# Moving the modulation products between the six sub-layers of a diffusion step

## The chip, the cores and the metric

The kernel runs on one core of a Trainium2 chip. The time is that of one execution on the device, in microseconds (us); several executions are timed and their median is given. One more execution was taken with the hardware profiler, and all rows below come from it. PE is TensorE (PEld its weight loads), DVE VectorE, ACT ScalarE, POOL GpSimd, and SP the engine whose queue issues nearly all of the DMA transfers.

## The reference

Two layers of a diffusion backbone, each with three sub-layers: a half-step SwiGLU feed-forward, a token mixer, and a second half-step feed-forward. There are 512 latent and 128 context tokens of width 1024, all in float32. The mixer of the first layer is a real 2-D Fourier transform over positions and channels (8 groups of 128 channels) between an input and an output projection; that of the second is a 16-head attention, dense among the context tokens and local in a grid for the latent ones. Each sub-layer is wrapped in norms whose shift, scale and gate come from a modulation vector:

```python
def _modulation(cond, w_mod, b_mod):
    m = jax.nn.silu(cond) @ w_mod + b_mod
    return m.reshape(cond.shape[0], N_MOD, D_MODEL)

def _modulated_prenorm(x, g, m, k):
    return _rmsnorm(x, g) * (1 + m[:, 3 * k + 1, None]) + m[:, 3 * k, None]
```

So each layer has nine modulation vectors of 1024 (three for each sub-layer), for two conditions (latent and context). The matrix `w_mod` of a layer is 1024 x 9216, 36 MB, and each of its numbers is used once for each condition. This work depends only on the two condition vectors and can be done at any time before the sub-layer that uses it.

## The kernel before, in words

All activations are kept transposed (128 channels on the partitions, tokens along the free axis) and the 640 tokens are handled as two halves of 320. For accuracy every float32 operand is split into a high part (ScalarE, a rounding copy, lines 190 and 200) and a low part (VectorE, the difference, lines 191 and 201), and each product is three matmuls, high x high, high x low, low x high: `mm3`, lines 206 to 208. In the trace a low part is thus a DVE row of L191 (a weight, 128x1024) or of L201 (an activation), and it must be there before its matmul.

Weights come as units of 512 KB (128x1024) by DMA into one of four buffers of the tag `raw` (`NRAW = 4`), are split into `hi` and `lo` tiles (six of each), and the buffer is free again after both. Units are requested in a fixed order (`unit`, three ahead). Tiles of one tag are handed out in program order. The order of instructions on each engine is laid down when the kernel is built: earlier lines of the program have priority, `high_priority` raises a few, and later work may run ahead where its operands and buffers are there. On the chip each engine then works through its list in that order.

The modulation vectors beyond the first two are cut into 128 jobs (`run`, line 1145). One job loads a 512 KB block of the transposed `w_mod` into a `raw` buffer, the same four buffers that the weights use, and has VectorE form two products, one for each condition:

```python
        for cond in conds:
            last = self.nc.vector.scalar_tensor_tensor(
                out=self.junk, in0=raw, scalar=1.0, in1=self.wide[:, cond, :],
                op0=ALU.mult, op1=ALU.mult, accum_out=self.mod[:, layer, cond, j : j + 1])
```

In the trace these are the DVE rows of L336 (`junk<-raw,wide`), and their loads the SP rows `raw<-in_w_mod_t`. Each eighth job adds the few 8-element operations of `coefs`. The jobs stand in one list, and `behind(n)` (line 194) takes the next n of them at that place of the program. Where it is called:

- In a feed-forward layer (`ffn`) the 22 blocks of hidden channels are cut into five slices (`SLICES`). After the first matrix of a slice come its 16 products with the second matrix (`w2`), eight output blocks for each half. `BEHIND[n]` jobs are spread evenly over the 64 `w2` steps of the first four slices (lines 654 to 658). Sub-layers 0, 2, 3 and 5 are feed-forward layers.
- In the Fourier sub-layer (n = 1, `fourier`), the input projection runs in four groups of four output blocks (first half, then second half), with two jobs after each. After each group of the second half `fold` prepares sums and differences of mirrored positions on VectorE (lines 784 to 789). Then come eight rounds, one for each channel group: `channels(g + 1)` (small float32 matmuls, lines 826 to 830; their result is split into the high part by ACT L200 and the low part by DVE L201, `ring<-score`) and `positions(g)` (twelve `mm3` matmuls with the transform matrices, then DVE L851 to L855 and a second split, `ring<-y`). After each of the first six rounds stands one job, and one more after each of the first six blocks of the first half of the output projection (`out_proj`).
- In the attention (n = 4, `attend`), 42 steps are woven between the projections' matmuls, and 24 of the first 33 steps carry a job.

Of the kernel before, what the change touches and what calls it, by code (L numbers as in the profile page):

```python
# [20 lines left out]
NCH = D // P  # L21
# [19 lines left out]
NBLK = 20  # L41
SLICES = ((0, 4), (4, 8), (8, 12), (12, 16), (16, 22))
FAST = range(4, NF - 2)
BEHIND = (28, 20, 28, 28, 24, 0)
BANKS = {"main": 4, "score": 2, "turn": 1, "sum": 1}
TEMPS = {"square": (2, TOK), "total": (2, TOK), "rms": (2, 3 * P), "left": (4, 384), "right": (3, 384)}

# [61 lines left out]
class Kernel:  # L109
# [371 lines left out]
    def ffn(self, layer, which, base, boundary):  # L481
# [3 lines left out]
        n = layer * 3 + 2 * which  # L485
        begun = [False, False]
        g, sums, kept = {}, {}, {}
# [6 lines left out]
        def w1(fs, half):  # L494
            for f in fs:
                if f not in g:
                    g[f] = self.ring(F32R).rearrange("p (a t) -> p a t", a=2)
            pss = []
            if fs[0] >= NF - 2:
                pss = [late(fs[0], j, half) for j in range(2)]  # L500
            elif len(fs) == 1:
                for j in range(2):
                    pss.append(self.proj(self.unit(base + self.w1_at[fs[0]] + j), lambda k: k * P, half,
                                         kind="score" if fs[0] == 2 else "main"))
            else:
                pss = self.multi([self.unit(base + self.w1_at[f] + j) for f in fs for j in range(2)], half)
            for i, f in enumerate(fs):
                gate, up = pss[2 * i], pss[2 * i + 1]
                s, v = self.temp("left"), self.temp("right")
                with self.tc.high_priority():  # L510
                    if f in kept and half:
                        for j, (to, ps) in enumerate(((s, gate), (v, up))):
                            nc.vector.tensor_tensor(to[:, :HALF], ps[:, :HALF], kept[f][j], op=ALU.add)
                        nc.scalar.activation(s[:, :HALF], s[:, :HALF], AF.Silu)
                        nc.vector.tensor_tensor(v[:, :HALF], v[:, :HALF], s[:, :HALF], op=ALU.mult)
                    else:
                        nc.scalar.activation(s[:, :HALF], gate[:, :HALF], AF.Silu)
                        nc.vector.tensor_tensor(v[:, :HALF], up[:, :HALF], s[:, :HALF], op=ALU.mult)  # L518
                    hidden(f, v, half)
                while self.later:  # L520
                    self.later.pop()()
# [23 lines left out]
        def combine(step):  # L545

            if step == 0:
                if n:
                    self.spilled = [self.dram.tile([P, 2 * TOK], F32, tag=f"spill{c}", name=self.name("spill"))
                                    for c in range(NCH // 2)]  # L550
                    for c in range(NCH // 2):
                        nc.sync.dma_start(out=self.spilled[c], in_=self.xs[n][c].rearrange("p c t -> p (c t)"))
                combine.now = {}
            k = step % 2 * 2
            b11, b12, b21, b22 = (self.pair(self.y, c, half) for c in (k, 4 + k) for half in (0, 1))
            if step < 2:
                t = combine.now[k] = [self.temp(("square", "total")[step]).rearrange("p (c t) -> p c t", c=2)
                                      for _ in range(2)]
                steps = ((1, t[0], b12, b11), (2, t[1], b22, t[0]))
            else:  # L560
                t = combine.now[k]
                steps = ((3, t[0], b22, b12), (4, t[1], t[1], b21))
            for i, to, a, b in steps:
                if k == 0:
                    sums[i] = [quad(self.ring(F32R)) for _ in range(2)]
                nc.vector.tensor_tensor(to, a, b, op=ALU.subtract)
                self.split(sums[i][0][:, k : k + 2, :], sums[i][1][:, k : k + 2, :], to)
# [48 lines left out]
        def seed(s, half, m):  # L616

            lo, hi = SPAN[half]
            ps = seeded[s, half, m] = self.bank()
            with self.tc.high_priority():  # L620
                nc.scalar.activation(ps[:, :HALF], self.y[:, m, lo:hi], AF.Copy)  # L621

        def w2(s, half, m):
            f0, f1 = SLICES[s]
            lo, hi = SPAN[half]
            ps = seeded.pop((s, half, m), None) or self.bank()
            for f in range(f0, f1):
                u, a = self.w2_tile(s, m, f - f0)
                w = self.unit(base + u)
                self.mm3(ps[:, :HALF], w[0][:, a : a + P], w[1][:, a : a + P],  # L630
                         g[f][:, 0, lo:hi], g[f][:, 1, lo:hi], f == f0 and s == 0, f == f1 - 1, s > 0)
            with self.tc.high_priority():
                nc.scalar.activation(self.y[:, m, lo:hi], ps[:, :HALF], AF.Copy)  # L633
            if f1 == NF:
                acc[half] = self.weigh(layer, 2 * which, half, m, acc[half])

        passed = done = 0
        adds = [(a[0], half, a[1]) for op, a, half in self.ffn_plan if op == "w2" and a[0]]
        for op, a, half in self.ffn_plan:
            if op == "w2" and a[0]:  # L640
                while adds and len(seeded) < 2 and adds[0][0] == a[0]:
                    seed(*adds.pop(0))
            if op == "w1":
                if not begun[half]:
                    self.finish(half)
                    begun[half] = True
                w1(a, half)
            elif op == "combine":
                combine(a)
            elif op == "fast":  # L650
                w1_fast(a)
            elif op == "w2":
                w2(a[0], half, a[1])
                if a[0] < len(SLICES) - 1:
                    passed += 1
                    due = BEHIND[n] * passed // (2 * NCH * (len(SLICES) - 1))
                    self.behind(due - done)
                    done = due
            elif op == "x":
                self.new_x(n + 1)  # L660
                for c in range(NCH // 2):
                    src = self.spilled[c].rearrange("p (c t) -> p c t", c=2) if n else self.io["x"][:, 2 * c : 2 * c + 2, :]
                    nc.sync.dma_start(out=self.xs[n + 1][c], in_=src)
            else:
                boundary(half, acc[half])
# [99 lines left out]
    def fourier(self, base, boundary):  # L765
# [38 lines left out]
        for half in (0, 1):  # L804
            lo, hi = SPAN[half]
            self.finish(half)
            for m0 in (0, 4):
                pss = self.multi([self.unit(base + m) for m in range(m0, m0 + 4)], half)
                with self.tc.high_priority():
                    for m, ps in zip(range(m0, m0 + 4), pss):  # L810
                        nc.scalar.activation(self.y[:, m, lo:hi], ps[:, :HALF], AF.Copy)
                if half:
                    fold(m0, nc.vector)
                self.behind(2)
        even_w, odd_w = self.unit(base + NCH), self.unit(base + NCH + 1)
        vs = {}

# [42 lines left out]
        for g in range(NCH):  # L860
            if g + 1 < NCH:
                channels(g + 1)
            positions(g)
            if g < 6:
                self.behind()
        self.out_proj(0, base + NCH + 2, boundary)

    def weave(self, parts, ns):
# [174 lines left out]
    def attend(self, pairs, ctx_qk, v):  # L1043
# [75 lines left out]
        for n in range(len(blocks) + 2):  # L1119
            parts = []  # L1120
            if 1 <= n <= len(blocks):
                parts.append(partial(scale, *blocks[n - 1]))
            if n < len(blocks):
                c, b = blocks[n]
                parts += [partial(ctx_scores if b == "c" else scores, c, b, p0) for p0 in range(2)]
            if n >= 2:
                parts.append(partial(take, *blocks[n - 2]))
            if 1 <= n <= len(blocks):
                parts += [partial(turn, *blocks[n - 1], p0) for p0 in range(2)]
            if n < 35 and (n % 5 < 3 or n in (3, 8, 13)):  # L1130
                parts.append(self.behind)
            steps.append(parts)
        return steps
# [143 lines left out]
```

## Time and profile before

| | us |
|---|---|
| median of 3 runs | 2336.14 (2333.36 to 2336.28) |
| the profiled execution's own time | 2334.2 |
| its span, first to last instruction | 2332.4 |
| PE busy | 2278.2 (98%) |
| PEld busy | 2225.2 (95%) |
| DVE busy | 1686.6 (72%) |
| ACT busy | 1270.9 (54%) |
| mean granted TensorE clock | 0.993 of full |

A busy engine is one that executes an instruction; a PE row's duration holds the time that the matmul spends in the pipeline, so consecutive rows overlap, and the rate is read from their starts. The share over the whole span is a mean over stages that differ: the Fourier sub-layer lies at about 480 to 650 us, the attention at about 1550 to 1830.

### The profile page before, as it was taken

The numbers are of one execution on the slowest core, as the hardware profiler recorded it, in microseconds if no ns is written. First come the engines' busy times: TensorE is split into PE (matmuls) and PEld (weight loads), VectorE is DVE, ScalarE is ACT, GpSimd is POOL, SyncE is SP. The second block draws the span as 40 slices with busy tenths as digits, with TensorE's granted clock in tenths as the row PEclk, the third lists the DMA queues.
The fourth block names the chain that finished last, engine by engine and source line by source line (L and its number), as shares of the span: only waits on it lengthen the run. The fifth ranks groups of instructions, "written<-read, shape, count | busy, mean of one in ns | idle before, by whom it ended". The sixth has DMA issues, their size and how long they took to land.

```text
span 2332.4 us, 39397 instructions
## 1 busy us (share of the span) xinstructions
PE 2278.2 (98%) x15756; PEld 2225.2 (95%) x15756; DVE 1686.6 (72%) x2934; ACT 1270.9 (54%) x2448; POOL 45.4 (2%) x64
## 2 busy tenths in 40 slices
PE   6999999998999999999999999999999999999997
PEld 4999999997999999999999999998888899999997
DVE  4878877389788877847878887378877485765553
ACT  4445545564653545556545555567767664545554
POOL 0000000000000000000000000010000000000000
PEclk9999999999999999999999999999999999999998
DMA  8234434334423433443234434224543212221241
GB/s 300 82 115 139 145 118 136 109 103 153 146 99 112 152 109 127 136 154 109 82 125 129 145 118 144 101 81 149 162 135 106 86 73 82 93 89 64 82 136 46
DMA packets 80280, 278.13 MB, mean 119 GB/s; under 512 B 8800, under 2 KB 15200, under 8 KB 79968
## 3 DMA queue, kind: packets, MB, share of 16 engines
q1 hardware_dynamic: 79824, 275.29, 36.1%
q8 instruction: 123, 2.02, 0.4%
q14 instruction: 61, 0.50, 0.1%
q10 hardware_dynamic: 272, 0.33, 0.0%
HBM read 264.04 MB, written 11.53 MB: 118 GB/s over the span
## 4 chain that ended last, share of the span: by engine, by line
PE 88%; DVE 5%; ACT 3%; DMA 3%; issue 1%; POOL 0%; SPq 0%; DVEq 0%; ACTq 0%; POOLq 0%
PE main L206 25%; PE main L208 25%; PE main L207 25%; PE score L206 3%; PE score L208 3%; PE score L207 3%; DVE junk L336 1%; PE sum L1108 1%; PE turn L1092 1%; PE sum L419 1%; DVE lo L191 1%; ACT hi L190 1%; PE score L1066 1%; DMA first<-in_w_mod_k 1%; DMA raw<-in_w_mod_t 1%
## 5 line engine op out<-in xcount | busy, mean ns | idle before, releaser
L206 PE MATMUL main<-ring,hi 128*128 128x320 f32 x3872 | 1204.5, 312 | 3.9 <-ACT ring L200 2.9
L208 PE MATMUL main<-ring,lo 128*128 128x320 f32 x3872 | 1198.0, 310 | 1.6 <-DVE lo L191 1.6
L207 PE MATMUL main<-ring,hi 128*128 128x320 f32 x3872 | 1198.9, 310 | 0.2 <-DVE ring L201 0.2
L206 PEld LDWEIGHTS main<-ring,hi 128*128 128x128 f32 x3872 | 727.7, 188 | 10.0 <-ACT ring L200 3.8
L208 PEld LDWEIGHTS main<-ring,lo 128*128 128x128 f32 x3872 | 727.6, 188 | 2.2 <-DVE lo L191 1.9
L207 PEld LDWEIGHTS main<-ring,hi 128*128 128x128 f32 x3872 | 728.1, 188 | 1.4 <-DVE ring L201 0.9
L190 ACT ACTIVATE hi<-raw 128x1024 fp32r<-128x1024 f32 (+1 forms) x358 | 350.3, 981 | 457.7 <-PE main L207 384.2
L191 DVE TENSOR_TENSOR lo<-raw,hi 128x1024 fp32r<-128x1024 f32 (+1 forms) x358 | 402.6, 1126 | 153.7 <-ACT hi L190 152.5
L336 DVE SCALAR_TENSOR_TENSOR junk<-raw,wide 128x1024 bf16<-128x1024 f32 x256 | 312.4, 1220 | 21.2 <-DMA raw<-in_w_mod_t 18.6
L633 ACT ACTIVATE y<-main 128x320 f32<-128x320 f32 x320 | 138.5, 433 | 172.3 <-PE main L208 170.9
L372 DVE TENSOR_TENSOR total<-total,square 128x640 f32<-128x640 f32 x71 | 58.3, 823 | 108.0 <-ACT square L371 106.1
L621 ACT ACTIVATE main<-y 128x320 f32<-128x320 f32 x256 | 111.9, 439 | 27.2 <-DVE left L607 10.5
L206 PE MATMUL score<-ring,hi 128*128 128x320 f32 x384 | 118.8, 309 | 0.0
L207 PE MATMUL score<-ring,hi 128*128 128x320 f32 x384 | 118.7, 309 | 0.0
L208 PE MATMUL score<-ring,lo 128*128 128x320 f32 x384 | 118.7, 309 | 0.0
L191 DVE TENSOR_TENSOR lo<-sums,hi 128x1024 fp32r<-128x1024 f32 x64 | 78.1, 1221 | 51.1 <-ACT hi L190 51.1
L206 PE MATMUL main<-ring,ring 128*128 128x320 f32 x352 | 110.5, 315 | 0.0
L208 PE MATMUL main<-ring,ring 128*128 128x320 f32 x352 | 108.9, 309 | 0.0
L207 PE MATMUL main<-ring,ring 128*128 128x320 f32 x352 | 108.7, 309 | 0.0
L190 ACT ACTIVATE hi<-sums 128x1024 fp32r<-128x1024 f32 x64 | 67.9, 1061 | 26.4 <-PE main L207 20.5
L200 ACT ACTIVATE ring<-right 128x320 fp32r<-128x320 f32 x112 | 51.6, 467 | 50.6 <-DVE right L518 40.6
L593 DVE TENSOR_TENSOR left<-left,main 128x320 f32<-128x320 f32 x64 | 31.2, 487 | 60.6 <-PE main L208 60.6
(181 smaller groups left out, 2676.1 us busy)
## 6 DMA issues: line engine op xcount, KB each, us to landing
raw<-in_w SPq DMA_DIRECT2D x264, 512.0 KB, 3.6
raw<-in_w_mod_t SPq DMA_DIRECT2D x128, 512.0 KB, 3.7
raw<-in_qkv SPq DMA_DIRECT2D x26, 512.0 KB, 3.7
first<-in_w_mod_k SPq DMA_DIRECT2D x16, 512.0 KB, 8.7
spill<-ring SPq DMA_DIRECT2D x12, 640.0 KB, 3.6
ring<-spill SPq DMA_DIRECT2D x12, 640.0 KB, 4.8
raw<-in_bias SPq DMA_DIRECT2D x16, 448.0 KB, 3.7
raw<-in_four_in SPq DMA_DIRECT2D x8, 512.0 KB, 3.5
```

What stands on the lines that cost most here:

```text
L190: nc.scalar.activation(hi, raw[:, at], AF.Copy)
L191: nc.vector.tensor_tensor(lo, raw[:, at], hi.bitcast(F32), op=ALU.subtract)
L200: self.nc.scalar.activation(hi, src, AF.Copy)
L206: mm(out, whi, xhi, start=start, stop=False)
L207: mm(out, whi, xlo, start=False, stop=False)
L208: self.latest = mm(out, wlo, xhi, start=False, stop=stop)
L336: last = self.nc.vector.scalar_tensor_tensor(out=self.junk, in0=raw, scalar=1.0, in1=self.wide[:, cond, :], op0=ALU.mult, op1=ALU.mult, ac ...
L372: nc.vector.tensor_tensor(acc, acc, sq, op=ALU.add)
L419: self.spread = nc.tensor.matmul(ps[:, t : t + P], col[:, j : j + 1].to_broadcast([P, P]), self.ident, start=True, stop=True)
L593: tt(a, q, z, op=ALU.subtract)
L621: nc.scalar.activation(ps[:, :HALF], self.y[:, m, lo:hi], AF.Copy)
L633: nc.scalar.activation(self.y[:, m, lo:hi], ps[:, :HALF], AF.Copy)
```

## The change

The jobs are the same and in the same order. Their places change: by sub-layer 36, 12, 28, 32, 12 and 8 instead of 28, 20, 28, 28, 24 and 0. In the feed-forward layers the steps of the last slice's first half take part too (72 steps instead of 64, but not in the last layer). In the Fourier sub-layer the input projection's groups carry none in the first half and three each in the second, the rounds none, the output projection six as before. In the attention every third step carries one.

```diff
-BEHIND = (28, 20, 28, 28, 24, 0)
+BEHIND = (36, 12, 28, 32, 12, 8)
...
                 w2(a[0], half, a[1])
-                if a[0] < len(SLICES) - 1:
+                if a[0] < len(SLICES) - 1 or half == 0:
                     passed += 1
-                    due = BEHIND[n] * passed // (2 * NCH * (len(SLICES) - 1))
+                    due = min(BEHIND[n], BEHIND[n] * passed // (2 * NCH * (len(SLICES) - 1) + (NCH if n < 5 else 0)))
                     self.behind(due - done)
                     done = due
...
                 if half:
                     fold(m0, nc.vector)
-                self.behind(2)
+                    self.behind(3)
...
             if g + 1 < NCH:
                 channels(g + 1)
             positions(g)
-            if g < 6:
-                self.behind()
...
-            if n < 35 and (n % 5 < 3 or n in (3, 8, 13)):
+            if n < 35 and n % 3 == 0:
                 parts.append(self.behind)
```

## Rows read from the trace of the kernel before

**Rows 1.** Stages: length; PE, PEld, DVE, ACT, POOL busy (instructions); clock; DMA share, GB/s.
```profile
37.00:482.00 445.00, 441.48 (x2999) 440.03 (x2999) 335.07 (x526) 234.49 (x414) 3.51 (x3) 0.99 0.38 124
482.00:544.00 62.00, 61.30 (x420) 60.49 (x419) 53.66 (x93) 29.61 (x54) 2.21 (x2) 1.00 0.37 117
544.00:582.00 38.00, 29.53 (x223) 26.37 (x222) 36.88 (x85) 20.16 (x50) 0.00 (x0) 0.91 0.41 132
...
1090.00:1548.00 458.00, 457.35 (x3131) 455.92 (x3130) 353.83 (x562) 243.96 (x444) 7.65 (x9) 1.00 0.39 125
...
1584.00:1820.00 236.00, 229.46 (x1771) 205.04 (x1770) 192.00 (x537) 177.17 (x463) 8.97 (x24) 1.00 0.46 144
...
1880.00:2332.00 452.00, 439.45 (x2988) 437.59 (x2987) 263.24 (x398) 225.74 (x405) 7.24 (x6) 0.99 0.25 83
```
**Rows 2.** The same view of the middle of the Fourier stage, in three pieces.
```profile
548.00:566.00 18.00, 15.06 (x127) 13.19 (x127) 17.63 (x43) 9.01 (x23) 0.00 (x0) 1.00 0.36 116
566.00:574.00 8.00, 4.40 (x36) 4.00 (x35) 8.00 (x21) 4.50 (x9) 0.00 (x0) 1.00 0.28 98
574.00:582.00 8.00, 6.07 (x31) 5.77 (x31) 7.25 (x19) 3.56 (x7) 0.00 (x0) 0.57 0.48 146
```
**Rows 3.** Waits in 525 to 600: total us, times, longest.
```profile
PE main L208 <- DVE ring L201: 8.0, 6, 1.9
```
**Rows 4.** VectorE's timeline: start, us, line, operation, tiles.
```profile
543.99 1.23 DVE L336 SCALAR_TENSOR_TENSOR junk<-raw,wide 128x1024 bf16<-128x1024 f32 x1
...
549.18 1.28 DVE L201 TENSOR_TENSOR ring<-score,ring 128x512 fp32r<-128x512 f32 x2
...
559.30 0.68 DVE L201 TENSOR_TENSOR ring<-score,ring 128x512 fp32r<-128x512 f32 x1
...
560.95 1.21 DVE L336 SCALAR_TENSOR_TENSOR junk<-raw,wide 128x1024 bf16<-128x1024 f32 x1
...
562.09 0.68 DVE L201 TENSOR_TENSOR ring<-y,ring 128x512 fp32r<-128x512 f32 x1
562.69 1.21 DVE L336 SCALAR_TENSOR_TENSOR junk<-raw,wide 128x1024 bf16<-128x1024 f32 x1
...
563.84 0.68 DVE L201 TENSOR_TENSOR ring<-score,ring 128x512 fp32r<-128x512 f32 x1
...
582.60 0.34 DVE L855 SCALAR_TENSOR_TENSOR ring<-main,col,ring 128x128 fp32r<-128x128 f32 x1
```
**Rows 5.** PE's timeline, in brackets the idle time before a row and its releaser.
```profile
544.46 0.47 PE L826 MATMUL score<-ring,y 128*128 128x128 f32 x2
...
549.91 0.39 PE L208 MATMUL main<-hi,ring 128*128 128x258 f32 x1 [0.28 <-DVE ring L201]
...
560.04 0.39 PE L208 MATMUL main<-hi,ring 128*128 128x258 f32 x1 [0.87 <-DVE ring L201]
...
562.95 0.27 PE L830 MATMUL turn<-ring,ring 128*63 128x128 f32 x1
564.57 0.39 PE L208 MATMUL main<-hi,ring 128*128 128x258 f32 x1 [1.35 <-DVE ring L201]
...
580.49 0.61 PE L206 MATMUL main<-ring,hi 128*128 128x320 f32 x1
```
**Rows 6.** SP's queue: start of the first, us to the last's end, loads, count.
```profile
506.06 27.81 SPq L155 DMA_DIRECT2D raw<-in_w_mod_t  x6
...
563.94 0.33 SPq L155 DMA_DIRECT2D raw<-in_four_out  x1
568.48 0.33 SPq L155 DMA_DIRECT2D raw<-in_w_mod_t  x1
```
**Rows 7.** Busy time: attention with jobs, without, and a burst of seven jobs.
```profile
1584.00:1784.00 200.00, 194.05 (x1497) 174.09 (x1496) 165.05 (x455) 144.39 (x377) 8.97 (x24) 1.00 0.47 148
1784.00:1820.00 36.00, 35.41 (x276) 30.95 (x276) 26.95 (x83) 32.78 (x87) 0.00 (x0) 1.00 0.40 127
108.00:148.00 40.00, 40.00 (x275) 40.00 (x274) 31.65 (x49) 16.39 (x29) 0.00 (x0) 1.00 0.41 132
```

## The prediction

> **What bounds the kernel now.** I read the stage windows first [rows 1]. In most stages TensorE (PE) is busy nearly all of the time at full clock: 441.5 of 445 us in the first feed-forward layer, 457.4 of 458 around the fourth sub-layer. So work that is added or removed on another engine there costs or gives nothing, as long as PE's inputs stay on time. The exceptions that the change touches are the middle of the Fourier stage (544 to 582: PE 29.5 of 38 us, clock 0.91, VectorE 36.9 of 38) and the attention (1584 to 1820: PE 229.5 of 236, VectorE 192).
>
> Then I cut the Fourier middle in three [rows 2]. PE is idle 2.9 of 18, 3.6 of 8 and 1.9 of 8 us, 8.5 us in all; in the last piece the granted clock averages 0.57 of full, which is mostly the lower of its two levels (1.2 instead of 2.4 GHz), after the emptiest piece. The 6.07 us of PE work there would take 6.07 x 0.57 = 3.5 us at full clock, so the clock costs another 2.6 us. The whole loss is about 11.1 us.
>
> The wait table says for whom: PE's matmul with the low part of the transformed channels waits for VectorE's subtraction that makes this low part, six times, up to 1.9 us [rows 3]. VectorE's own timeline shows why it is late [rows 4]. From one such subtraction (559.30) to the next (563.84) are 4.54 us, and in them stand two modulation products of 1.14 us each from start to start. Without them a group costs VectorE 4.54 - 2.28 = 2.26 us. PE's timeline gives the other side [rows 5]: from the late matmul at 560.04 to the last matmul of the same round at 562.95 are about 3.1 us of work, and the next round starts at 564.57. So the round is set by VectorE with its products (4.54), would be set by PE without them (3.1), and VectorE would then have 0.8 us to spare in each round.
>
> **The change, part by part.** All 128 jobs remain, each one load of 512 KB, two products and, every eighth time, a few tiny operations. By sub-layer they go from 28, 20, 28, 28, 24, 0 to 36, 12, 28, 32, 12, 8. Only places change.
>
> *Fourier middle, six jobs fewer (8 positions rounds).* If nothing took their place, VectorE would need 8 x 2.26 = 18.1 us for what it now does from 549.18 to 582.9, and PE would bind. PE can't get all 11.1 us back: the fold of the second half of the channels stands in front of the first low part on VectorE, which starts at 549.18 [rows 4], and it stays. PE began at 544.46, and its matmul with the first low part starts at 549.91 after 0.28 us of idle time [rows 5]; counting short stalls between unlike matmuls, I take 4 us of its work as done by then. Of 8 rounds 8 x 3.1 - 4 = 20.8 us remain, with two small sums some 21.2, which from 549.9 end at 571.1, against 580.49 now, when the next matmuls begin [rows 5]. The upper bound is 9.4 us.
>
> The gap does not stay empty, though. Six jobs still follow in the output projection, and the build-time planner lets later work run ahead where an engine is free. What limits it is the four load buffers, handed out in program order. Now the projection's weights and jobs alternate in that order: a weight load at 563.94, a job load at 568.48 [rows 6]. With six jobs gone ahead of them, these loads move to the front. Two of the weights will hold a buffer until the transform matrices release their split copies, so one or two buffers keep turning over. I count the first job done before the fold and two or three inside the rounds, with two splits of projection weights (1.14 us each, as long as a product). VectorE then needs, from 549.2:
> with two jobs 18.1 + 2 x 2.28 + 2.3 = 25.0 us, that is to 574.2, 8.7 us earlier than now (582.9), close to PE's own bound;
> with three 27.2 us, 6.4 earlier; with four 29.5 us, 4.2 earlier; with five 31.8 us, 1.9 earlier.
> A job that is planned into a true gap costs only the part of a product by which it delays the next subtraction, and PE uses each low part one round later. I take 7.0 us back, between two jobs and three, with bounds of 1.9 and 9.4.
>
> The page "TensorE: Matmul & The Clock Gate" of the Trainium skill (section on a second failure mode, cycling through result banks) says that frequent short idles between matmul groups can be enough to make the clock swing. In this trace the clock was 1.00 through 18 us with 2.9 us of short idles [rows 2], which speaks against it for what I leave idle; by the rule the sum would be 2.6 us less.
>
> *Fourier, input projection, eight jobs become six.* The two after each of the first half's groups go, and three instead of two follow each of the second half's. In this stretch PE loses 0.7 of 62 us [rows 1], with VectorE 54 us busy; two jobs less are worth 0 to 0.7, I take 0.3. The three jobs that follow the second fold have an earlier place in the program than the rounds, so they would stand in front of them if their loads were late. Now six loads went through in 27.8 us from 506.06 while three buffers were held by weights [rows 6], and the eighth job's last product ends at 545.2 [rows 4]. Six jobs in the same room, with a free start, end some 5 us or more before that.
>
> *Attention, 24 jobs become 12.* PE is idle 5.95 of 200 us (3.0%) where jobs run and 0.59 of 36 (1.6%) in the last part, where none does [rows 7]. Half the jobs gone is worth about half of the difference, 0.7% of 200 = 1.3 us. Most of what PE waits for there is ScalarE's copy of a transposed block, to which VectorE only contributes, so the bounds are 0 and 5.
>
> *Feed-forward layers.* The first gets 32 jobs instead of 28 beside its first four slices of the second matrix, the last gets 8 where it had none; the first, third and fourth sub-layers get four jobs each in the first half of the last slice, for which the third gives up four elsewhere. I cost this at nothing. What hides it: in one burst of seven jobs (108 to 148) VectorE is busy 31.7 of 40 us and PE all 40 [rows 7]; an eighth job brings 2.4 us. The last layer has VectorE 263 of 452 us busy [rows 1]; 8 jobs add 20. The extra loads go through the same four buffers ahead of the next stage's weights, which wait for the release of split copies anyway. If that cover failed, each of the 40 added products that stood in front of a weight split would cost PE up to 1.22 us.
>
> *Sum.* 7.0 + 0.3 + 1.3 + 0 = 8.6 us. The profiled execution's own time was 2334.2 (span 2332.4 and 1.8 around it); it would become 2325.6. The median of the three runs is 2336.1, 1.9 above it; I forecast from that: 2327.5.
>
> **Rivals.**
> (a) *The projection's jobs refill the rounds.* Four or five come forward, and VectorE stays the bound: 1.9 to 4.2 us back, with the other parts 3.5 to 5.8: 2330.3 to 2332.6, say 2331.5. For it: the planner's willingness to run ahead, and the buffers that become free. Against it: they come last in priority, and two buffers are held by weights.
> (b) *The clock still falls.* Short idles from the remaining products take it to the lower level for some 6 us of work, as now: 2.6 us, so 2330.1. The page on the clock gate named above describes such a swing. Against it: the 18 us at 1.00 [rows 2].
> (c) *The attention gives more*, because its order is laid out anew with VectorE a tenth less busy: up to 5 us, and the rounds reach PE's bound: 9.4 + 0.3 + 5 = 14.7, so 2321.4.
> (d) *Nothing that can be measured.* The three jobs behind the second fold come late and stand in front of the rounds: 6 x 1.14 = 6.8 us at the start cancels the 7.0: 2336.1 - 1.8 = 2334.3. Against it: the rate of loads [rows 6].
> (e) *Slower: the products that moved are exposed in the feed-forward layers.* In-order VectorE holds a weight split behind a product, PE waits up to 1.22 us for each. It decides from 8.6 / 1.22 = 7 of the 40 products on; with 15 exposed, 18.3 - 8.6 gives 2345.8. Against it: 168 products run there now, in three layers, with PE idle 0.1% to 0.8% of the time [rows 1].
>
> **How the numbers follow.** This kernel's measurement can tell about 0.2%, 4.7 us, from no change: faster means under 2331.5, slower over 2340.8. Chances: forecast 0.55 (2324 to 2331), (a) 0.17, (b) 0.05, (c) 0.08, (d) 0.08, (e) 0.07. Of (a) a little under half is under 2331.5. So faster 0.55 + 0.05 + 0.08 + 0.07 = 0.75, same 0.10 + 0.08 = 0.18, slower 0.07. The range goes from 2320.5 (all of (c), a little below its end) to 2334 (all of (a), a part of (d)) and leaves out (e) and most of (d), less than 0.2.
>
> **What would show it.** Right: the stage from the first channel transform to the output projection's first matmul shrinks from 36.0 us to about 29; the wait of PE for the low part falls from 8.0 us to under 3; the granted clock stays 1.00 there; one round takes 3.1 to 3.5 us; two or three jobs stand among the rounds. In the attention PE's idle time falls from 6.5 to about 5 us. The feed-forward layers keep their lengths within 0.5 us. Wrong: a VectorE still full of products in the rounds (a), a lower clock there with short idles (b), products at 545 to 552 (d), or new waits of PE for weight splits in the first or last feed-forward layer (e).

## The result and the profile after

The changed kernel takes 2320.43 us (median of 4 runs, 2320.17 to 2321.61) against 2336.21 us (4 runs, 2333.36 to 2336.65): a ratio of 0.9936 (95% interval 0.9919 to 0.9953), 15.8 us in medians where 8.6 were forecast. The profiled execution took 2321.61 us (span 2319.8), 12.6 less than the one before; the working below goes by these two.

The stages of the changed kernel, in the columns of [rows 1]; the third line is the middle of the Fourier stage, the fifth the attention:

```profile
37.00:480.00 443.00, 439.56 (x2975) 438.06 (x2976) 351.03 (x556) 230.64 (x407) 3.51 (x3) 0.99 0.41 133
480.00:546.00 66.00, 65.99 (x454) 65.20 (x453) 53.03 (x89) 33.83 (x65) 1.70 (x2) 1.00 0.35 107
546.00:573.00 27.00, 26.23 (x214) 23.42 (x213) 23.89 (x60) 17.71 (x47) 0.00 (x0) 1.00 0.25 79
1080.00:1538.00 458.00, 457.36 (x3130) 455.92 (x3128) 363.71 (x577) 244.40 (x443) 8.51 (x9) 1.00 0.40 129
1574.00:1808.00 234.00, 226.80 (x1775) 205.45 (x1774) 166.32 (x487) 178.04 (x464) 8.74 (x24) 1.00 0.37 119
1868.00:2320.00 452.00, 438.88 (x2988) 437.02 (x2986) 281.34 (x434) 225.54 (x405) 7.16 (x6) 0.99 0.28 93
```

In the Fourier middle PE is now busy 26.23 of 27 us at clock 1.00, where it had 29.5 of 38 at 0.91 [rows 1]: the loss is gone, and with it the lower clock. The feed-forward stages show that nothing was paid for it: around the fourth sub-layer PE is busy 457.36 of 458 (457.35 before) although VectorE has 10 us more to do, and in the last layer 438.88 of 452 (439.45) although VectorE does 18 us more.

PE's timeline of the rounds (columns as in [rows 5]) shows the ends and the only idle time in between:

```profile
545.33 0.47 PE L826 MATMUL score<-ring,y 128*128 128x128 f32 x2
...
548.82 0.39 PE L206 MATMUL main<-hi,ring 128*128 128x258 f32 x1 [0.78 <-ACT ring L200]
...
571.97 0.41 PE L206 MATMUL main<-ring,hi 128*128 128x320 f32 x1
```

From the first channel transform to the output projection's first matmul are 26.6 us instead of 36.0 [rows 5]. No matmul waits for VectorE's low part any more; PE is idle once, 0.78 us, for ScalarE's first high part.

VectorE's timeline of the same stretch (columns as in [rows 4]) shows how it came about:

```profile
545.41 1.22 DVE L336 SCALAR_TENSOR_TENSOR junk<-raw,wide 128x1024 bf16<-128x1024 f32 x1
...
547.70 1.20 DVE L784 TENSOR_TENSOR ring<-y 128x1008 f32<-128x1008 f32 x1
...
550.60 1.28 DVE L201 TENSOR_TENSOR ring<-score,ring 128x512 fp32r<-128x512 f32 x2
551.79 1.22 DVE L191 TENSOR_TENSOR lo<-raw,hi 128x1024 fp32r<-128x1024 f32 x1
552.93 1.22 DVE L336 SCALAR_TENSOR_TENSOR junk<-raw,wide 128x1024 bf16<-128x1024 f32 x1
...
557.98 0.68 DVE L201 TENSOR_TENSOR ring<-score,ring 128x512 fp32r<-128x512 f32 x1
559.17 0.69 DVE L201 TENSOR_TENSOR ring<-y,ring 128x512 fp32r<-128x512 f32 x1 [0.51 <-ACT ring L200]
...
560.83 0.68 DVE L201 TENSOR_TENSOR ring<-score,ring 128x512 fp32r<-128x512 f32 x1
562.27 0.69 DVE L201 TENSOR_TENSOR ring<-y,ring 128x512 fp32r<-128x512 f32 x1 [0.76 <-ACT ring L200]
...
563.92 0.68 DVE L201 TENSOR_TENSOR ring<-score,ring 128x512 fp32r<-128x512 f32 x1
...
572.15 1.22 DVE L336 SCALAR_TENSOR_TENSOR junk<-raw,wide 128x1024 bf16<-128x1024 f32 x1
```

A round now takes 2.85 to 3.1 us (557.98, 560.83, 563.92), and VectorE has 0.5 to 0.8 us to spare in some of them, in which it waits for ScalarE. One single product stands among the rounds (552.93); the next, the other one of the same job, comes when they are over (572.15). That isn't for want of data: SP's queue (columns as in [rows 6]) issued two job loads ahead of and among the last weights:

```profile
544.26 0.33 SPq L155 DMA_DIRECT2D raw<-in_w_mod_t  x1
546.67 0.33 SPq L155 DMA_DIRECT2D raw<-in_four_out  x1
547.80 0.33 SPq L155 DMA_DIRECT2D raw<-in_w_mod_t  x1
553.07 0.33 SPq L155 DMA_DIRECT2D raw<-in_four_out  x1
573.40 0.33 SPq L155 DMA_DIRECT2D raw<-in_w_mod_t  x1
```

Laid side by side by the starts of the same matmuls, the 12.6 us of the traces come about as follows. The first feed-forward layer ends 1.6 us later than before. The input projection with the norm ahead of it takes 66.4 instead of 67.1 us (-0.7), the rounds to their last matmul 26.6 instead of 36.0 (-9.4), the rest of the Fourier stage loses 0.5. From there to the attention's entry the offset moves by 0.3 in 970 us. The attention, from its first score matmul to the last matmul that takes values, is 238.5 instead of 241.2 (-2.7), and 0.6 go behind it. The sum is -12.6. The 1.6 us at the start belong to the execution: between 40 and 60 us the granted clock was 0.94 before and 0.86 after, the whole 1.6 us are there by 58 us, and in the five experiments below with the same first layer it ended 0.3 to 1.6 us later than before.

The attention is the surprise. PE's waits in it (us in total, times, longest) are no fewer than before. The largest of them, first of the kernel before, then of the changed one:

```profile
PE turn L1092 <- ACT right L1094: 5.0, 11, 1.2
```

```profile
PE turn L1090 <- ACT right L1092: 6.1, 14, 0.8
```

PE's idle time there did not fall: 7.2 of 234 us above, 6.5 of 236 in [rows 1]. What shrank is the time in which PE counts as busy; the experiments show that this column hides short waits.

### The profile page after: what moved, and what is told of

It reads as the page before. It is cut to its first block, busy times and chain, and to the rows that moved or that the text cites. A ratio compares the mean times of both kernels' runs of the same rounds, so it can differ in the third digit from the quotient of the medians.

```text
span 2319.8 us, 39404 instructions
## 1 busy us (share of the span) xinstructions
PE 2273.3 (98%) x15756; PEld 2224.0 (96%) x15756; DVE 1689.8 (73%) x2934; ACT 1270.9 (55%) x2448; POOL 43.7 (2%) x64
## 4 chain that ended last, share of the span: by engine, by line
PE 89%; ACT 4%; DVE 3%; DMA 2%; issue 1%; POOL 0%; SPq 0%; DVEq 0%; ACTq 0%; POOLq 0%
PE main L206 26%; PE main L207 25%; PE main L208 25%; PE score L206 3%; PE score L208 3%; PE score L207 3%; PE turn L1090 1%; PE sum L419 1%; PE sum L1106 1%; DVE lo L191 1%; ACT hi L190 1%; DMA first<-in_w_mod_k 1%; PE score L1064 1%; PE sum L410 1%; DMA raw<-in_w 1%
## 5 line engine op out<-in xcount | busy, mean ns | idle before, releaser
L206 PEld LDWEIGHTS main<-ring,hi 128*128 128x128 f32 x3872 | 727.8, 188 | 10.3 <-ACT ring L200 3.9
L621 ACT ACTIVATE main<-y 128x320 f32<-128x320 f32 x256 | 111.8, 439 | 30.9 <-DVE left L607 12.1
```

The source lines that it names most:

```text
L206: mm(out, whi, xhi, start=start, stop=False)
```

## The experiments

Two questions stood open. Was it the products' time on VectorE that held up the rounds, or their loads and buffers? And why did the attention give twice what was forecast, with no less idle time? Each run is compared with runs of the kernel before on the same chip, whose medians were 2335.54, 2335.3, 2335.48 and 2334.55 us in the four groups of runs. The lengths of rounds (first channel transform to last position matmul, 36.0 us before, 26.6 after) and attention (241.2 and 238.5) are read from each run's trace.

### What held up the rounds

*Rounds only.* The kernel before, its six jobs of the rounds moved to the first feed-forward layer.

```diff
-BEHIND = (28, 20, 28, 28, 24, 0)
+BEHIND = (34, 14, 28, 28, 24, 0)
...
-            if g < 6:
-                self.behind()
```

> Kernel before, only the six jobs of the Fourier rounds taken out and put into the first feed-forward layer (34 instead of 28 over its 64 steps). Theory A (VectorE's products set the rounds): the stage from the first channel transform to the output projection's first matmul shrinks from 36.0 to about 26.5 us, clock 1.00 there, and the kernel takes 9 to 10 us less than before, about 2326.5. Rival B (most of the 15.8 us between the medians come from elsewhere, from the attention or the input projection): under 6 us less.

It took 2325.29 us, 10.3 less than before, 0.9958 (0.9945 to 0.9972); rounds 26.1 us, attention 241.1.

*The loads stay, the products go.* The kernel before; the six jobs of the rounds load their blocks but form no products (12 products are left out).

```diff
-                        self.gemv(self.raw_tile(self.io["w_mod_t"][layer, j]), layer, j)
+                        raw = self.raw_tile(self.io["w_mod_t"][layer, j])
+                        if not (layer == 0 and 52 <= j < 58):
+                            self.gemv(raw, layer, j)
```

> Kernel before, but the six jobs that stand in the Fourier rounds only load their blocks; their twelve products are left out (those modulation values are then wrong). Theory A (VectorE's time): as if the jobs were gone, 9 to 10 us less than before. Rival C (the loads and the buffers that they hold make the rounds late): within 3 us of before.

2324.8 us, 10.7 less than before, 0.9956 (0.9943 to 0.9968); rounds 26.6 us.

*One product of the two.* As before it, with the product for the first condition kept (6 products are left out).

```diff
+                        self.gemv(raw, layer, j, (0,) if layer == 0 and 52 <= j < 58 else (0, 1))
```

> Kernel before, but each of the six jobs in the Fourier rounds forms only the product of the first condition; six products are left out. Theory A with PE as the second bound: a round needs VectorE 2.26 + 1.14 = 3.40 us against PE's 3.1, so the rounds lose only 0.3 us each: 6 to 8 us less than before, clock 1.00 in the rounds. If each product costs the same wherever PE stands: half of the whole gain, 4.5 to 5.

2326.53 us, 9.0 less than before, a little more than expected, 0.9962 (0.995 to 0.9975); rounds 28.3 us. Its windows row for them:

```profile
545.00:574.00 29.00, 26.12 (x216) 23.41 (x215) 28.57 (x71) 18.14 (x46) 0.00 (x0) 1.00 0.51 162
```

It is the products' time, and neither loads nor buffers: with the loads in place and no product the rounds are about as short (26.6) as with the jobs moved away (26.1, and 26.6 in the changed kernel). And it is a matter of two engines' bounds, not a slope. The first product of a round costs little (26.6 to 28.3 us, 0.3 us a round over six rounds), the second much (28.3 to 36.0, 1.3 us a round, with the lower clock of [rows 2] in it). That is what the prediction's sum for one round says: VectorE with one product 2.26 + 1.14 = 3.4 us against PE's 3.1, with two 4.54. In the row above VectorE is full (28.57 of 29), PE is idle 2.9 us, and the clock stays at 1.00.

### What shortened the attention

*Attention alone* (the kernel before with the change's attention, its feed-forward places for the freed jobs, and the Fourier stage as it was), and its opposite, *attention undone* (the changed kernel with the 24 jobs back in their places):

```diff
-BEHIND = (28, 20, 28, 28, 24, 0)
+BEHIND = (28, 20, 28, 32, 12, 8)
...
-            if n < 35 and (n % 5 < 3 or n in (3, 8, 13)):
+            if n < 35 and n % 3 == 0:
```

```diff
-BEHIND = (36, 12, 28, 32, 12, 8)
+BEHIND = (36, 12, 28, 28, 24, 0)
...
-            if n < 35 and n % 3 == 0:
+            if n < 35 and (n % 5 < 3 or n in (3, 8, 13)):
```

> Changed kernel with the whole Fourier sub-layer and the first layer's count as before (28, 20, 28, 32, 12, 8). Theory A (products on VectorE delay the softmax chain): 3 to 4 us less than before. Prediction's own estimate: 1.3 us less. Rival N (chance of the laid-out order): anything between 2 us more and 4 us less, without relation to the number of products.

> Changed kernel with the attention's 24 jobs at their old steps (fourth sub-layer 28, last layer 0), all else as changed. If attention, fourth and last sub-layer are worth the 3.4 us that the two traces show between the attention's start and end: 12 us less than before, about 2324. If they are worth nothing beyond chance: as the changed kernel, about 15.8 us less than before.

Alone: 2332.41 us, 0.9987 (0.9979 to 0.9996), attention 238.95 us, rounds 35.3. Undone: 2323.11 us, 0.9947 (0.9935 to 0.996), attention 241.6, rounds 26.6. The two parts add up, and the attention's is 2.3 to 3.1 us of its own stretch.

*No jobs in the attention* (the changed kernel, `BEHIND = (36, 12, 28, 44, 0, 8)` and the two lines with `self.behind` taken out of `attend`), *the 12 jobs in other steps* (`n < 36 and n % 3 == 1`), and *the 24 jobs as before without products* (the kernel before; the last 24 jobs of the second layer load but form no products, 48 products are left out):

> Changed kernel with no job in the attention; its twelve go to the fourth sub-layer (44 instead of 32). Theory A: the attention gains as much again as from 24 to 12 jobs, 3 to 4 us, so 18 to 20 us less than before, if the fourth sub-layer hides the twelve. Rival N: no further gain, 14 to 16 us less. If the fourth sub-layer can't hide 44 jobs, PE waits there for low parts of weights and its length grows beyond 458 us.

> Changed kernel with the attention's twelve jobs at every third step, but one step later (1, 4, 7 and so on). Theory A: as the changed kernel within 1.5 us. Rival N: several us away from it, either way.

> Kernel before, but the 24 jobs of the attention only load their blocks; their 48 products are left out (those modulation values are then wrong). Theory A (VectorE's time): the attention gains what taking all 24 jobs away would, 6 to 8 us less than before. Rival C (loads, buffers, or the order of the queue): within 2 us of before.

None: 2321.24 us, 0.9939 (0.9927 to 0.9952), attention 238.45. Shifted: 2322.2 us, 0.9943 (0.993 to 0.9957), attention 239.3. Without products: 2333.08 us, 0.9991 (0.9982 to 0.9999), attention 238.9. So the gain does not grow with the work taken off VectorE: from 24 jobs to 12 gives 2.7 us, from 12 to none nothing, and 48 products gone with the jobs' places kept give no more than 24 gone. In the attention the shifted jobs stayed within the 1.5 us that theory A allowed (0.8). But it asked another 3 to 4 us of the run without jobs, which gave none, and 6 to 8 of the one without products, which gave 2.2.

These lengths alone do not rule out a delay by VectorE that ends at some number of jobs below 24, as the second product's did in the rounds. But then ScalarE should wait less for VectorE's small results of the softmax (`col`: row maxima, reciprocals of sums) when half the jobs are gone. It waits 26.8 us for them before and 31.3 after, by these rows (us in total, times, longest):

```profile
ACT left L1052 <- DVE col L1069: 13.7, 9, 2.8
ACT left L1086 <- DVE col L1053: 9.1, 15, 2.0
...
ACT left L1052 <- DVE col L1080: 4.0, 2, 3.0
```

```profile
ACT left L1050 <- DVE col L1067: 19.0, 15, 2.7
...
ACT left L1050 <- DVE col L1078: 8.2, 4, 3.6
...
ACT left L1084 <- DVE col L1051: 4.1, 8, 1.4
```

What does go with the length is the order that was laid out for PE. The matmuls that take the values (`take`, L1108 before, L1106 after, the rows `sum<-right`) are narrow and stand between those of the projections in groups, runs of this line with no other in between. Counted from PE's order, the kernel before has 52 such groups, and so have the other four kernels with its attention (240.2 to 241.6 us); the shifted one has 49 (239.3), the one without products 48 (238.9), and the changed kernel, attention alone and the one without jobs 47 (238.45 to 238.95). The changes between all kinds of matmul do not tell these kernels apart: 379 in the attention before, 378 after. Jobs and products are part of what the layout is made from: each job is one of the pieces that `weave` spreads evenly among the matmuls, and what VectorE is given decides when the pieces behind it are ready. One such group in the changed kernel's timeline of PE:

```profile
1701.70 0.31 PE L207 MATMUL main<-ring,hi 128*128 128x320 f32 x1
1701.85 0.31 PE L208 MATMUL main<-ring,lo 128*128 128x320 f32 x1
1702.09 0.44 PE L1106 MATMUL sum<-right,square 128*64 128x128 f32 x4
1702.46 0.42 PE L206 MATMUL main<-ring,hi 128*128 128x320 f32 x1
1702.72 0.31 PE L207 MATMUL main<-ring,hi 128*128 128x320 f32 x1
1702.87 0.31 PE L208 MATMUL main<-ring,lo 128*128 128x320 f32 x1
```

Two projection matmuls start 0.15 us after each other; the group starts 0.24 after the last one, and behind it the second start is 0.26 after the first. Going over and back costs about 0.2 us, and none of it is shown as idle time.

*The order made worse with the same work.* To test this, `take` was given the first priority among what is ready, once in the kernel before (24 jobs) and once in the changed kernel (12 jobs); both then have 79 groups.

```diff
+        def first(what, *a):
+            with self.tc.high_priority():
+                what(*a)
...
-                parts.append(partial(take, *blocks[n - 2]))
+                parts.append(partial(first, take, *blocks[n - 2]))
```

> The kernel before with all its 24 attention jobs in their places; the matmuls that take the values with the probabilities only get the first priority among what is ready, so TensorE goes over to them in 79 separate groups instead of 52. Order theory (going over to these narrow matmuls and back costs about 0.2 us each time beyond the matmuls themselves): 27 groups more cost at least 27 x 0.2 = 5.4 us, the attention takes 246 to 252 us instead of 241.2, the kernel 2341 to 2347, with the same work on VectorE. Load theory (the attention's length follows how full VectorE is with products): VectorE's work is the same, so 241 us within 1.

> The changed kernel (12 attention jobs) with the same first priority for the matmuls that take the values: also 79 groups. Order theory: with the number of groups held equal, 12 jobs instead of 24 give under 1 us in the attention against the kernel with 24 jobs and 79 groups. Load theory: the attention is again 2.5 to 3 us shorter with 12 jobs than with 24 and 79 groups.

With 24 jobs: 2347.68 us, 1.0052 (1.0039 to 1.0064), attention 253.3. With 12: 2338.61 us, 1.0013 (1.0004 to 1.0022), attention 255.8. The windows rows of the attention, first of the kernel before, then with 24 jobs and 79 groups, then with 12 and 79:

```profile
1586.00:1827.00 241.00, 234.03 (x1806) 207.89 (x1806) 191.52 (x540) 179.88 (x471) 8.97 (x24) 1.00 0.45 142
```

```profile
1586.50:1839.50 253.00, 243.44 (x1805) 212.62 (x1805) 192.62 (x540) 179.22 (x471) 9.54 (x24) 1.00 0.43 135
```

```profile
1576.00:1831.50 255.50, 243.09 (x1806) 212.81 (x1806) 164.72 (x488) 180.85 (x471) 8.88 (x24) 1.00 0.34 109
```

The load theory falls as it was stated: VectorE has the same work in the first two rows (191.5 and 192.6 us), and the attention is 12 us longer; it has 28 us less in the third than in the second, and the attention is no shorter. So the order laid out for PE can by itself make the attention longer. The size was underestimated: 246 to 252 us was the range.

The 12.1 us are 0.45 for each of the 27 groups more, but that is not the price of going over. Much of it is waiting, which PE's column shows as busy (243.44 against 234.03): a projection matmul's row lasts 0.31 us and the next starts 0.15 after it, so a wait of up to 0.16 us behind it leaves no idle time. The weight loads (PEld) show these waits. With the first priority, `take` stands in PE's order before ScalarE has copied the probabilities; its weight loads wait for that, in the kernel before and in the same with 79 groups:

```profile
PEld sum L1108 <- ACT right L1094: 1.7, 5, 0.6
```

```profile
PEld sum L1108 <- ACT right L1094: 20.4, 52, 1.1
```

The transposes' waits for these copies (10.3 us before) nearly go in return. All waits of weight loads for ScalarE in these two windows add up to 15.7 and 23.2 us (without one at the very start, for `rms`). So, as an estimate, 7.5 of the 12.1 us are waiting, and the 4.6 that are left, 0.17 a group, lie near the 0.2 of the single group above. By 0.2 a group the 5 groups fewer of the change are worth about 1.0 us of its 2.7; the weight loads' waits for ScalarE are 1.2 us less than before (14.5); 0.5 stays open. No run changes the number of groups and leaves those waits as they are, so this split is not shown by experiment. The third kernel's extra 2.5 us go with waits of PE for the same copies, in the order of these two kernels 7.7 and 11.0 us:

```profile
PE sum L1108 <- ACT right L1094: 7.7, 17, 0.8
```

```profile
PE sum L1106 <- ACT right L1092: 11.0, 19, 1.0
```

*The order made better.* The changed kernel, with the pieces of a step that need PE (two scores, `take`, the first transposes) entered as one piece. The groups of `take` are 46; counting all kinds of matmul, PE goes from one kind to another 269 times in the attention instead of 378.

```diff
+        def together(group):
+            for part in group:
+                part()
...
+            group = []
+            if n < len(blocks):
+                group = [parts.pop(-2), parts.pop(-1)]
             if n >= 2:
-                parts.append(partial(take, *blocks[n - 2]))
+                group.append(partial(take, *blocks[n - 2]))
+            if 1 <= n <= len(blocks):
+                group.append(partial(turn, *blocks[n - 1], 0))
+            if group:
+                parts.append(partial(together, group))
             if 1 <= n <= len(blocks):
-                parts += [partial(turn, *blocks[n - 1], p0) for p0 in range(2)]
+                parts.append(partial(turn, *blocks[n - 1], 1))
```

> The changed kernel with the same 12 attention jobs; of each block's pieces, the two score matmul pairs, the matmuls that take the values of the block two before and the first transposes are entered as one piece instead of four, so that TensorE goes from one kind of matmul to another 269 times in the attention instead of 378; the groups that take the values are 46, as good as the 47 of the changed kernel. If every change of kind costs (about 0.08 us for a way back, as the first matmul after a transpose shows), 109 fewer give up to 9 us: attention 230 to 236 us, kernel 2312 to 2318. If only the groups that take the values count, the attention stays at 238.5 within 1 us and the kernel at 2320 to 2323. If the pieces now meet the single transpose bank or a probability copy before ScalarE is done, the waits of TensorE for ScalarE's copy grow past 6.1 us and the attention is longer than 240 us.

2317.91 us (2317.54 to 2318.72), 0.9928 (0.9914 to 0.9942), attention 235.0, the shortest of all. Its windows row of the attention, and the changed kernel's by the same ends:

```profile
1577.00:1812.00 235.00, 227.47 (x1803) 205.85 (x1803) 164.91 (x489) 177.79 (x471) 8.14 (x24) 1.00 0.38 120
```

```profile
1576.50:1815.00 238.50, 230.99 (x1806) 207.91 (x1807) 165.21 (x488) 180.84 (x471) 8.74 (x24) 1.00 0.36 117
```

In PE's column the 3.5 us are all busy time; it is idle 7.5 us in both. The groups of `take` are 47 and 46 and can't account for them. The 109 changes of kind fewer cost at most 3.5 / 109 = 0.03 us on average instead of the 0.08 of the expectation, and probably less, since the waits fell too: all waits of weight loads for ScalarE from 14.5 to 10.4 us (for VectorE they rose from 0.4 to 1.7), and those of the transposes, first of the changed kernel, then of this one, to half:

```profile
PEld turn L1090 <- ACT right L1092: 11.6, 22, 1.0
```

```profile
PEld turn L1090 <- ACT right L1092: 5.7, 11, 0.9
```

By the ratios this kernel and the changed one can't be told apart (the intervals overlap); by the traces the attention is shorter.

### Whether the feed-forward layers hide every job

*All jobs there.* None in the Fourier stage and none in the attention: `BEHIND = (48, 0, 28, 44, 0, 8)` in the kernel without attention jobs, with the calls of `behind` taken out of the input and the output projection too.

> All 48 jobs of the first layer run in its first feed-forward layer, none in the Fourier stage; none in the attention, 44 in the third feed-forward layer, 8 in the last. If products are hidden wherever TensorE is the bound, the feed-forward layers keep their lengths within 0.5 us, the input projection gives up to 0.7 us more, the attention and the rounds are as in the changed kernel: 2319 to 2322. If products that move there are exposed at up to 1.22 us each, the first and third feed-forward layer are 5 us and more longer and the kernel takes 2326 or more.

2322.11 us, 0.9939 (0.9925 to 0.9952). The fourth sub-layer with 44 jobs is as long as with 28 or 32 (394.2 to 394.7 us between the same two norms). The first with 48 takes 409.1 us from its norm to the next one. With 36 jobs it takes 408.1 to 408.3 in the four kernels in which the clock stayed at 1.00 from there on, as it did here (409.6 and 409.7 in the two in which it fell once more near 52 us). So some 0.9 us do show, more than the 0.5 allowed. They were lost between 263 and 337 us of the trace, where PE's weight loads wait twice for VectorE's results in the first matrix (`left`), 1.1 us in all; in the changed kernel they do not wait there. The windows row of 300 to 340, in which the changed kernel has PE busy 40.00 and VectorE 32.22 us:

```profile
300.00:340.00 40.00, 39.44 (x267) 38.92 (x266) 36.03 (x62) 19.26 (x31) 0.00 (x0) 1.00 0.39 127
```

The input projection with its norm takes 65.9 us; with six jobs it took 66.3 to 66.4 in all six kernels, with eight 67.0 to 67.1 in all seven. The whole Fourier stage is 1.3 us shorter than in the changed kernel, which the first layer's 0.9 nearly takes back. It gains nothing that can be measured over the change: next to nothing is left to move.

## Why the prediction was right, and where it was not

- *Fourier rounds, 7.0 us forecast, 9.4 measured.* The mechanism was right: the product-less rounds run at PE's bound. The term was mis-sized in one step, "I count the first job done before the fold and two or three inside the rounds". One product came forward, not two or three jobs, though loads had landed and VectorE had gaps, and with it the upper bound held to a tenth: it put the next matmuls at 571.1; they began at 571.97, 0.87 of which the stage started later. The experiment with one product per round shows why even that was too cautious: a job in the form of one product a round costs 0.3 us, since PE's bound stands close by.
- *Input projection, 0.3 forecast, 0.7 measured*, the upper end given, and the same in every kernel with six jobs there. The step that the six jobs end "some 5 us or more" before 545 failed: the last product ended at 546.6, 1.1 us ahead of the fold. It delayed nothing on PE's side.
- *Attention, 1.3 forecast, 2.7 measured, for a wrong reason.* The step "Half the jobs gone is worth about half of the difference" of PE's idle shares failed. The idle time did not fall, ScalarE waited no less for VectorE, and with 79 groups half the jobs gave nothing. That "its order is laid out anew", which stood only in rival (c), is what fits: five fewer groups and fewer waits for ScalarE's copies, an estimated 2.2 of the 2.7 us. That order alone moves the attention by more than this is shown; that it is the whole cause of these 2.7 us is argued. That a new order would be better and not worse could not have been read from the profile: this part was luck.
- *Feed-forward layers, 0 forecast.* Right: 40 more products, and no stage but the first moved by more than 0.2 us; the first by its clock at the start. With 12 jobs more in the first layer about 0.9 us show.
- *The sum.* 8.6 forecast, 12.6 in the traces: 2.4 from the rounds, 0.4 from the input projection, 1.4 from the attention, 1.4 between and behind these stages that had no term, less 1.6 at the start. The medians add 3.2, because the execution profiled before lay 2.0 under its median and the one after 1.2 over it. So the forecast's own band (2324 to 2331) was missed by 3.6 us, and the median of 2320.43 lies at the very end of the stated range, 2320.5 to 2334: all three terms were taken too small.
- *The rivals.* (c) had the time (2321.4) and both its conditions, at a chance of 0.08, which was too low: that the rounds would reach PE's bound was, by the rows, as likely as the refill. (a) did not come: the planner did not refill. (d) did not: the three jobs of the last group had formed their products by 546.6, ahead of the second fold. (e) did not; with all 48 jobs of the first layer in its feed-forward layer, 24 products more than in the change, it begins to show, at 0.9 us. (b), the swing of the clock that the Trainium skill describes ("TensorE: Matmul & The Clock Gate", the section on a second failure mode): the clock was 1.00 in the changed rounds, which hardly test it, and also in the run with one product a round, with 2.9 of 29 us idle in short pieces, which does; the rule did not show here. In [rows 2] it fell after a stretch with 3.6 of 8 us idle.

## What to carry to other kernels

Where a side engine shares a loop with TensorE, add up both for one round: side work is free until its sum passes TensorE's, and the piece that passes it costs about its whole length, so moving half of it can give nearly all. Where several streams of matmuls are woven by a planner, an edit of the pieces, even of pieces for other engines, can lay the order out anew: compare the order before and after, and the waits of the weight loads, since short waits and the going over between matmuls show as busy time of PE. The mere number of changes of kind does not tell (379 and 378 here). Where TensorE is the bound for hundreds of microseconds, side work in VectorE's free time costs nothing until VectorE is nearly full: here nothing at 36 jobs in the first layer, about 0.9 us at 48.

## What the hardware showed that was not expected

Going from the projections' matmuls (128x320) to the narrow ones that write 64 partitions and back costs about 0.2 us by their starts, all of it inside rows that count as busy. Waits of up to 0.16 us behind a projection matmul count as busy too. So the same matmuls in another order take 227 to 243 us of busy PE at a clock of 1.00 throughout, while their weight loads are busy 206 to 213 us.
